# Second parts of weight pieces: by an accumulating transfer instead of a subtraction on VectorE

## The chip, the cores and the metric

The kernel runs on one core of one Trainium2 chip. The metric is the device time of one execution in microseconds (us), lower is better. Before the change the median of three runs is 1182.73 us (1181.46 to 1182.98).

## What is computed

A two-layer decoder trunk on 512 tokens of width 1024, all in float32. Cut to what matters:

```python
# layer 0
proj = x @ w_in                                  # q | k | v | g | a low-rank gate
o = gla_chunked(q, k, v, log_a)                  # 4 heads, gated linear attention
mix = (rms_norm(o) * norm_g * silu(g)) @ gla_w_o
# layer 1: 16 heads of 64, weights by stick-breaking
kv = h @ kv_w;  q = h @ sb_w_q
mix = stick_breaking_attention(q, k, v) @ sb_w_o
# both layers
h = layer_norm(ALPHA * h + mix)
h = layer_norm(ALPHA * h + relu(h @ w_up) ** 2 @ w_down)   # D_FF = 4096
```

## The kernel before

Matmuls run in a reduced-precision format (F32R), so each operand x is kept as two parts: a first part hi, which is x rounded to F32R, and a second part lo = x - hi. A product is then three matmuls: hi with hi, hi with lo, lo with hi (mm3, L91 to 95, and the loop at L306 in the multiplications described next). The work is cut into weight pieces of 128 partitions by 1024 columns, 512 KB. For each piece SyncE loads the raw weights (L64), ScalarE writes hi with a copy (L70), VectorE writes lo with a subtraction (L72). The tiles come from pools: three raw buffers, six hi and six lo. A piece can be made only when the matmuls of the piece six before it have read their buffers, so ScalarE's hi copy normally starts when TensorE lets a buffer go.

Three shapes of use follow. pieces_512 gives four pieces (two for half a weight), each two blocks of 128 rows by 512 columns; piece_128 gives one piece of eight blocks of 128 by 128. In the up half of the MLP (function up) TensorE goes through a piece once, 24 matmuls. In a row product (function rows, for values and gates) TensorE goes through all four pieces of a group once per block of tokens, four times, so the four are released together near the end of the group. The output products of the first mixer and of both MLPs (function seven) use seven products of sub-blocks instead of eight. Their weights are loaded ahead in eight B tiles (L266), which VectorE combines with each other in place (L335, L336, L346, L347). Six of the seven products take such tiles, two pieces each, of which the first two, split_b(2) and split_b(3) of L337 and L343, use tiles that are still plain weights. The other one, plain_b, loads its two pieces anew through raw. There are nine such multiplications, eight of them in the MLPs.

In the attention the heads go in eight pairs. GpSimd multiplies each of five weight tiles of a pair (w, L770) with the result of a scan on VectorE (r, L769), and copies keys across partitions (kh, L737). LayerNorm takes means and variances on VectorE, a power on GpSimd (rs, L185), the centring on VectorE (h, L189), and then TensorE transposes (L213) for the next product.

The code names no order between engines: a recording layer orders the instructions of each engine by its own estimate of when their inputs are ready, and inserts the waits. Each engine works its queue strictly in that order. GpSimd's queue also holds any DMA that it issues. In the lines below a name with a number, as in L72, is a line of the kernel before.

Of the kernel before, what the change touches and what calls it, by code (L numbers as in the profile page):

```python
# [8 lines left out]
F32 = mybir.dt.float32  # L9
F32R = mybir.dt.float32r  # L10
I32 = mybir.dt.int32
AF = mybir.ActivationFunctionType
ALU = mybir.AluOpType
# [21 lines left out]
def yoco_kernel(ctx: ExitStack, tc: tile.TileContext, x, gla_w_in, gla_w_a2, gla_b_a, gla_norm_g,  # L35
                gla_w_o, kv_w, sb_w_q, sb_w_o, mlp_w_up, mlp_w_down, ln_g, ln_b, out):
    nc = tc.nc
# [10 lines left out]
    def nm(s):  # L48
        uid[0] += 1
        return f"{s}{uid[0]}"  # L50

    def bank():
        return psp.tile([P, 512], F32, tag="b", name=nm("ps"))

    def row_tile():
        return big.tile([P, D], F32, tag="h", bufs=4, name=nm("h"))

    def unit(dtype):
        return big.tile([P, 4, 512], dtype, tag="T", bufs=8, name=nm("T"))


    def split_piece(src, a):
        raw = wts.tile([P, 1024], F32, tag="raw", bufs=3, name=nm("raw"))
        nc.sync.dma_start(out=raw.rearrange("p (a b) -> p a b", a=a), in_=src)  # L64
        return split_tile(raw, a)

    def split_tile(raw, a):
        v = lambda w: w.rearrange("p (a b) -> p a b", a=a)
        hi = wts.tile([P, 1024], F32R, tag="hi", bufs=6, name=nm("hi"))
        nc.scalar.activation(hi, raw, AF.Copy)  # L70
        lo = wts.tile([P, 1024], F32R, tag="lo", bufs=6, name=nm("lo"))
        nc.vector.tensor_tensor(lo, raw, hi.bitcast(F32), op=ALU.subtract)  # L72
        return v(hi), v(lo)

    def block(w, r0, c0):
# [21 lines left out]
    def put(hi, lo, ps, keep=lambda ins: ins):  # L97
        keep(nc.scalar.activation(hi, ps, AF.Copy))  # L98
        keep(nc.vector.tensor_tensor(lo, ps, hi.bitcast(F32), op=ALU.subtract))  # L99
# [154 lines left out]
    def seven(a1, a2, weights, pool, hs, fresh, norms=False, mid=None, narrow=False):  # L254
# [6 lines left out]
        a11, a21, a12, a22 = a1[:, :, lo_t], a1[:, :, hi_t], a2[:, :, lo_t], a2[:, :, hi_t]  # L261
        bs = []
# [9 lines left out]
        def split_a(a):  # L272
            u = unit(F32R)
            put(u[:, :, lo_t], u[:, :, hi_t], a)
            return lambda k, s: (u[:, k, 128 * s:128 * s + 128], u[:, k, 256 + 128 * s:384 + 128 * s])

        def split_b(i):
            got = []
            for h in range(2):
                hi, lo = split_tile(bs[h][i], 2)  # L280
                got += [(hi[:, 0, :], lo[:, 0, :]), (hi[:, 1, :], lo[:, 1, :])]
            return got

# [9 lines left out]
        ys, xs, zs = ([None, None] for _ in range(3))  # L293
# [28 lines left out]
        def product(*how, **more):  # L322
            for s in range(2):
                part(s, *how, **more)
# [9 lines left out]
        for b22, b12, b11, b21 in bs:  # L334
            tt(b22, b22, b12, op=ALU.subtract)  # L335
            tt(b12, b12, b11, op=ALU.subtract)  # L336
        product(split_a(a11), split_b(2), ys, True, False, 0, 0)  # L337
        if mid:
            mid()
            sums()  # L340
        q12 = split_a(a12)
        tt(a21, a11, a21, op=ALU.subtract)
        product(q12, split_b(3), xs, True, True, 0, 0, last=True)  # L343
        tt(a12, a12, s2, op=ALU.subtract)
        for b22, b12, b11, b21 in bs:
            tt(b11, b22, b11, op=ALU.add)  # L346
# [52 lines left out]
    xs, pss = [row_tile() for _ in range(NT)], [bank() for _ in range(NT)]  # L399
# [8 lines left out]
    for u in range(2):  # L408
        for t in range(NT):
            nc.sync.dma_start(out=xs[t][:, 512 * u:512 * u + 512],  # L410
                              in_=x2[128 * t:128 * t + 128, 512 * u:512 * u + 512])
# [3 lines left out]
            raw, hi, lo = (w[:, 512 * (t % 2):512 * (t % 2) + 512] for w in trio)  # L415
            k = 4 * u + t
# [185 lines left out]
    op = tc.tile_pool(name="gated", bufs=1, reuse_waits="tile")  # L602
# [120 lines left out]
    class Pair:  # L723
# [23 lines left out]
        def weights(self):  # L747

            self.ws = []
            for kind, segs in ((0, ((0, 3, 0),)), (1, ((0, 2, 0), (0, 0, 384))), (0, ((1, 3, 0),)),  # L750
                               (1, ((1, 2, 0), (1, 0, 384))), (2, ((0, 1, 0), (1, 1, 256)))):
                z = bank()
                for a, i, f in segs:
                    q = self.qs[:, a, P * i:P * i + P]
                    n = P * (i + 1)
                    for k, end in ((self.kh, False), (self.kl, True)):
                        nc.tensor.matmul(z[:, f:f + n], lhsT=q, rhs=k[:, a, 0:n], start=not end, stop=end)

                z4 = z.rearrange("p (b c) -> p b c", c=P)
                last = (z4[:, 3:4, :], z4[:, 2:4, :], z4[:, 1::2, :])[kind]  # L760
                nc.vector.tensor_tensor(last, last, low.unsqueeze(1).broadcast_to([P, last.shape[1], P]), op=ALU.add)  # L761
                r = sbp.tile([P, S + 1], F32, tag="r", bufs=3, name=nm("r"))
                w = chain()
                nc.gpsimd.memset(r[:, S:S + 1], 1.0)
                rb = r[:, 0:S]
                nc.scalar.activation(rb, z, AF.Sigmoid, scale=-1.0)
                nc.scalar.activation(w, z, AF.Sigmoid)
                down = rb[:, ::-1]
                nc.vector.tensor_tensor_scan(down, down, begins[kind][:, ::-1], 1.0, op0=ALU.mult, op1=ALU.max)  # L769
                nc.gpsimd.tensor_tensor(w, w, r[:, 1:S + 1], op=ALU.mult)  # L770
                self.ws.append((segs, w))
# [116 lines left out]
```

## Time and profile before

| | |
|---|---|
| median of 3 runs | 1182.73 us |
| the profiled execution's own time | 1182.95 us |
| its span, first to last instruction | 1181.0 us |
| TensorE busy | 1137.2 us (96%) |
| VectorE busy | 877.0 us (74%) |
| ScalarE busy | 546.5 us (46%) |
| GpSimd busy | 96.2 us (8%) |
| DMA engines' share by loads | 32.5% of 16 engines' span, 120.96 MB |

The profile is of one execution. PE is TensorE's matmuls, PEld its weight loads, DVE VectorE, ACT ScalarE, POOL GpSimd, SPq SyncE's queue, which issues the loads. A row of the groups names line, engine, operation, tiles (out<-in), shapes and count, then busy time in us and the mean in ns, then the engine's idle time just before, and what ended it. A row of the waits reads: who waited, for whom, us in total, times, longest. A row of the timeline starts with the start and the duration in us. A row of the DMA issues ends with the size and the median time from issue to landing.

### The profile page before, as it was taken

To read this page: it belongs to the slowest core of one execution; us is meant where nothing else is said; L and a number is where in the kernel's file an instruction comes from. 1 tells how busy PE (TensorE), PEld (TensorE's weight loads), DVE (VectorE), ACT (ScalarE), POOL (GpSimd) and SP (SyncE) were. 2 spreads that over 40 slices of the span, in tenths; PEclk is the share of its full clock that TensorE was granted. 3 is DMA by queue.
4 is the path that set the end of the run, shared out by engine and by line. 5 is a ranking of instruction groups with operands and counts; after the bars stand their busy time and mean duration, and the time that the engine had idled before them with its cause. 6 is when DMAs were issued, how large, how long until landed. Compare 5 with 4: busy or idle time off the path is not lost.

```text
span 1181.0 us, 14039 instructions
## 1 busy us (share of the span) xinstructions
PE 1137.2 (96%) x5401; PEld 934.0 (79%) x5401; DVE 877.0 (74%) x1053; ACT 546.5 (46%) x807; POOL 96.2 (8%) x159
## 2 busy tenths in 40 slices
PE   8999999799999999998799999999999999999986
PEld 7788887598888888886588877778988888888865
DVE  4577558985877857968953787786958768679697
ACT  4455435553433524534643667664544435345250
POOL 1011100000000000000010443431000000000001
PEclk9999998899999999998899999999999999999988
DMA  7441341272351450421243311111732614515101
GB/s 229 121 125 54 99 134 54 88 238 103 102 183 36 142 164 33 162 71 36 72 129 106 87 41 67 55 54 36 234 123 87 193 42 129 174 34 163 54 1 71
DMA packets 87846, 121.84 MB, mean 103 GB/s; under 512 B 11298, under 2 KB 37026, under 8 KB 87780
## 3 DMA queue, kind: packets, MB, share of 16 engines
q1 hardware_dynamic: 87780, 120.96, 32.5%
q8 instruction: 42, 0.69, 0.2%
q14 instruction: 24, 0.20, 0.1%
HBM read 118.85 MB, written 2.10 MB: 102 GB/s over the span
## 4 chain that ended last, share of the span: by engine, by line
PE 78%; DVE 15%; ACT 3%; issue 2%; POOL 1%; DMA 0%; SPq 0%; DVEq 0%; POOLq 0%; ACTq 0%
PE ps L306 26%; PE ps L93 16%; PE ps L94 16%; PE ps L95 16%; DVE r L769 4%; DVE lo L72 3%; ACT wt L784 1%; DVE T L99 1%; DVE h L168 1%; ACT hi L70 1%; DVE bst L176 1%; DVE ps L761 1%; DVE qs L744 1%; PE ps L213 1%; POOL rs L185 1%
## 5 line engine op out<-in xcount | busy, mean ns | idle before, releaser
L306 PE MATMUL ps<-hi,T 128*128 128x512 f32 (+1 forms) x1016 | 326.7, 399 | 16.4 <-ACT T L98 7.0
L93 PE MATMUL ps<-T,hi 128*128 128x512 f32 (+1 forms) x768 | 288.7, 376 | 0.0
L95 PE MATMUL ps<-T,lo 128*128 128x512 f32 (+1 forms) x768 | 285.5, 372 | 0.0
L94 PE MATMUL ps<-T,hi 128*128 128x512 f32 (+1 forms) x768 | 285.4, 372 | 0.0
L306 PEld LDWEIGHTS ps<-hi,T 128*128 128x128 f32 x1016 | 195.5, 194 | 64.6 <-ACT T L98 8.1
L72 DVE TENSOR_TENSOR lo<-raw,hi 128x1024 fp32r<-128x1024 f32 x134 | 163.0, 1225 | 111.3 <-ACT hi L70 107.6
L70 ACT ACTIVATE hi<-raw 128x1024 fp32r<-128x1024 f32 x134 | 142.6, 1065 | 191.7 <-PE ps L306 90.1
L306 PE MATMUL ps<-lo,T 128*128 128x512 f32 (+1 forms) x508 | 201.4, 396 | 0.0
L70 ACT ACTIVATE hi<-B 128x1024 fp32r<-128x1024 f32 x108 | 114.5, 1060 | 171.7 <-PE ps L94 99.4
L72 DVE TENSOR_TENSOR lo<-B,hi 128x1024 fp32r<-128x1024 f32 x108 | 131.1, 1222 | 64.1 <-ACT hi L70 63.5
L95 PEld LDWEIGHTS ps<-T,lo 128*128 128x128 f32 x768 | 144.7, 188 | 25.0
L93 PEld LDWEIGHTS ps<-T,hi 128*128 128x128 f32 x768 | 144.7, 188 | 24.6 <-issue 1.1
L94 PEld LDWEIGHTS ps<-T,hi 128*128 128x128 f32 x768 | 144.8, 189 | 23.5
L306 PEld LDWEIGHTS ps<-lo,T 128*128 128x128 f32 x508 | 98.4, 194 | 19.6
L93 PE MATMUL ps<-hi,T 128*128 128x512 f32 x256 | 103.1, 404 | 0.0
L95 PE MATMUL ps<-hi,T 128*128 128x512 f32 x256 | 100.8, 394 | 0.0
L94 PE MATMUL ps<-lo,T 128*128 128x512 f32 x256 | 100.8, 394 | 0.0
L168 DVE TENSOR_TENSOR h<-ps,h 128x512 f32<-128x512 f32 x109 | 74.6, 686 | 13.6 <-PE ps L306 9.5
L185 POOL TENSOR_TENSOR rs<-ve,mhalf 128x1 f32<-128x1 f32 x16 | 12.2, 760 | 814.2 <-DVE ve L183 814.2
L769 DVE TENSOR_TENSOR_SCAN r<-r,begin 128x512 f32<-128x512 f32 x40 | 66.2, 1663 | 0.2
L660 DVE TENSOR_TENSOR s<-ps,s 128x512 f32<-128x512 f32 x64 | 43.3, 688 | 19.4 <-ACT s L659 19.4
L770 POOL TENSOR_TENSOR w<-w,r 128x512 f32<-128x512 f32 x40 | 51.4, 1285 | 75.7 <-DVE r L769 60.5
(164 smaller groups left out, 1223.7 us busy)
## 6 DMA issues: line engine op xcount, KB each, us to landing
raw<-in_mlp_w_up_dram SPq DMA_DIRECT2D x64, 512.0 KB, 3.8
B<-in_mlp_w_down_dram SPq DMA_DIRECT2D x64, 512.0 KB, 4.0
raw<-in_gla_w_in_dram SPq DMA_DIRECT2D x20, 512.0 KB, 3.9
raw<-in_mlp_w_down_dram SPq DMA_DIRECT2D x16, 512.0 KB, 3.9
raw<-in_kv_w_dram SPq DMA_DIRECT2D x16, 512.0 KB, 3.9
B<-in_gla_w_o_dram SPq DMA_DIRECT2D x8, 512.0 KB, 7.2
raw<-in_sb_w_q_dram SPq DMA_DIRECT2D x8, 512.0 KB, 4.3
raw<-in_sb_w_o_dram SPq DMA_DIRECT2D x8, 512.0 KB, 3.5
```

What stands on the lines that cost most here:

```text
L70: nc.scalar.activation(hi, raw, AF.Copy)
L72: nc.vector.tensor_tensor(lo, raw, hi.bitcast(F32), op=ALU.subtract)
L93: nc.tensor.matmul(ps, lhsT=a[0], rhs=b[0], start=first, stop=False)
L94: nc.tensor.matmul(ps, lhsT=a[0], rhs=b[1], start=False, stop=False)
L95: nc.tensor.matmul(ps, lhsT=a[1], rhs=b[0], start=False, stop=last)
L99: keep(nc.vector.tensor_tensor(lo, ps, hi.bitcast(F32), op=ALU.subtract))
L168: nc.vector.tensor_tensor(h, ps, h, op=ALU.add)
L185: nc.gpsimd.tensor_tensor(rs, ve, mhalf[:, 0:1], op=ALU.pow)
L306: nc.tensor.matmul(banks[s][:, c], lhsT=a(k, s)[x], rhs=b[k][y][:, c], start=opens and (k, x, y) == (0, 0, 0), stop=closes and (k, x, y) = ...
L660: nc.vector.tensor_tensor(s2[:, f, :], pss[f], s2[:, f, :], op=ALU.mult)
L769: nc.vector.tensor_tensor_scan(down, down, begins[kind][:, ::-1], 1.0, op0=ALU.mult, op1=ALU.max)
L770: nc.gpsimd.tensor_tensor(w, w, r[:, 1:S + 1], op=ALU.mult)
```

## The change

Second parts of plain weights are no longer subtracted on VectorE. ScalarE writes a second copy of the raw weights, with the sign turned, into lo; since lo is an F32R tile, this is -hi. Then GpSimd issues a DMA that reads the same weights from memory again and adds them to lo in place, so that lo = weights - hi. This is done for all pieces through raw tiles (134) and for the two products of each of the nine multiplications whose B tiles are still plain (36 pieces). The other 72 B pieces, which VectorE has combined, keep the subtraction.

```diff
     def split_piece(src, a):
         raw = wts.tile([P, 1024], F32, tag="raw", bufs=3, name=nm("raw"))
         nc.sync.dma_start(out=raw.rearrange("p (a b) -> p a b", a=a), in_=src)
-        return split_tile(raw, a)
-
-    def split_tile(raw, a):
+        return split_tile(raw, a, src)
+
+    def split_tile(raw, a, src=None):
+
         v = lambda w: w.rearrange("p (a b) -> p a b", a=a)
         hi = wts.tile([P, 1024], F32R, tag="hi", bufs=6, name=nm("hi"))
         nc.scalar.activation(hi, raw, AF.Copy)
         lo = wts.tile([P, 1024], F32R, tag="lo", bufs=6, name=nm("lo"))
-        nc.vector.tensor_tensor(lo, raw, hi.bitcast(F32), op=ALU.subtract)
+        if src is not None:
+            nc.scalar.activation(lo, raw, AF.Copy, scale=-1.0)
+            nc.gpsimd.dma_start(out=v(lo), in_=src, accum_op=ALU.add)
+        else:
+            nc.vector.tensor_tensor(lo, raw, hi.bitcast(F32), op=ALU.subtract)
         return v(hi), v(lo)
...
-        def split_b(i):
+        def split_b(i, *block):
             got = []
             for h in range(2):
-                hi, lo = split_tile(bs[h][i], 2)
+                k, j = block or (0, 0)
+                hi, lo = split_tile(bs[h][i], 2, weights(k, h, j) if block else None)
                 got += [(hi[:, 0, :], lo[:, 0, :]), (hi[:, 1, :], lo[:, 1, :])]
             return got
...
-        product(split_a(a11), split_b(2), ys, True, False, 0, 0)
+        product(split_a(a11), split_b(2, 0, 0), ys, True, False, 0, 0)
...
-        product(q12, split_b(3), xs, True, True, 0, 0, last=True)
+        product(q12, split_b(3, 1, 0), xs, True, True, 0, 0, last=True)
```

The new instructions stand in the queues of ScalarE and GpSimd, and some old ones change places. First ScalarE's queue in the first MLP, at the end of a multiplication of seven products: the two pieces of plain_b (raw_2764, raw_2770), the last B pieces, and the first pieces of the next up group. Before:

```order
L70 ACTIVATE hi_2766<-raw_2764 128x1024
L70 ACTIVATE hi_2772<-raw_2770 128x1024
L98 ACTIVATE T_2802<-s_2287 128x4x256
L70 ACTIVATE hi_2805<-B_2578 128x1024
L70 ACTIVATE hi_2809<-B_2586 128x1024
L98 ACTIVATE T_2813<-s_2420 128x4x256
L70 ACTIVATE hi_2816<-B_2584 128x1024
L70 ACTIVATE hi_2820<-B_2592 128x1024
L70 ACTIVATE hi_2878<-raw_2876 128x1024
L70 ACTIVATE hi_2884<-raw_2882 128x1024
```

And now (the same raw tiles are numbered 2806, 2813 and 2920):

```order
L74 ACTIVATE lo_2810<-raw_2806 128x1024
L71 ACTIVATE hi_2808<-raw_2806 128x1024
L71 ACTIVATE hi_2815<-raw_2813 128x1024
L74 ACTIVATE lo_2817<-raw_2813 128x1024
L103 ACTIVATE T_2846<-s_2317 128x4x256
L71 ACTIVATE hi_2849<-B_2616 128x1024
L71 ACTIVATE hi_2853<-B_2624 128x1024
L103 ACTIVATE T_2857<-s_2454 128x4x256
L71 ACTIVATE hi_2860<-B_2622 128x1024
L71 ACTIVATE hi_2864<-B_2630 128x1024
L74 ACTIVATE lo_2924<-raw_2920 128x1024
L71 ACTIVATE hi_2922<-raw_2920 128x1024
```

A lo copy has come beside each hi copy of a raw piece; of two pieces that follow each other, the first has its lo copy ahead of its hi copy and the second behind it. The B pieces here are combined ones, and have none.

Next GpSimd's queue in the attention, from the fourth and fifth w of one head pair over the copies of keys (kh) to the first products of the next. Before:

```order
L770 TENSOR_TENSOR w_5019<-w_5019,r_5018 128x512
L764 MEMSET r_5200 128x1
L770 TENSOR_TENSOR w_5032<-w_5032,r_5031 128x512
L764 MEMSET r_5211 128x1
L737 COPY kh_5105<-kh_5105 64x512 x2
L770 TENSOR_TENSOR w_5188<-w_5188,r_5187 128x512
L764 MEMSET r_5224 128x1
L770 TENSOR_TENSOR w_5201<-w_5201,r_5200 128x512
L764 MEMSET r_5237 128x1
```

And now:

```order
L770 MEMSET r_5307 128x1
L75 DMA lo_5581<-in_sb_w_q_dram 128x8x128
L743 COPY kh_5200<-kh_5200 64x512
L75 DMA lo_5729<-in_kv_w_dram 128x8x128
L743 COPY kh_5200<-kh_5200 64x512
L776 TENSOR_TENSOR w_5284<-w_5284,r_5283 128x512
L770 MEMSET r_5320 128x1
L776 TENSOR_TENSOR w_5297<-w_5297,r_5296 128x512
L770 MEMSET r_5333 128x1
L75 DMA lo_5768<-in_sb_w_q_dram 128x8x128
L776 TENSOR_TENSOR w_5308<-w_5308,r_5307 128x512
```

Transfers stand between the two kh copies and ahead of the third w (in this pair, the first of its kind, also ahead of the kh copies; in the pairs behind it only at the other two places).

Last GpSimd's queue at the LayerNorm behind the first mixer, four token blocks, each with one power rs. Before:

```order
L185 TENSOR_TENSOR rs_1848<-ve_1846,mhalf 128x1
L185 TENSOR_TENSOR rs_1869<-ve_1867,mhalf 128x1
L185 TENSOR_TENSOR rs_1951<-ve_1949,mhalf 128x1
L185 TENSOR_TENSOR rs_2011<-ve_2009,mhalf 128x1
L185 TENSOR_TENSOR rs_4365<-ve_4363,mhalf 128x1
```

And now:

```order
L190 TENSOR_TENSOR rs_1874<-ve_1872,mhalf 128x1
L75 DMA lo_2073<-in_mlp_w_up_dram 128x2x512
L190 TENSOR_TENSOR rs_1895<-ve_1893,mhalf 128x1
L75 DMA lo_2080<-in_mlp_w_up_dram 128x2x512
L75 DMA lo_2087<-in_mlp_w_up_dram 128x2x512
L75 DMA lo_2094<-in_mlp_w_up_dram 128x2x512
L190 TENSOR_TENSOR rs_1977<-ve_1975,mhalf 128x1
L75 DMA lo_2330<-in_mlp_w_up_dram 128x2x512
L190 TENSOR_TENSOR rs_2037<-ve_2035,mhalf 128x1
```

The second to fourth rs now stand behind transfers, each of which waits for its own lo copy on ScalarE.

## The prediction

> **What bounds the kernel now.** I read the page's busy line first, then the waits of TensorE, then busy time by stretch.
>
> ```profile
> span 1181.0 us, 14039 instructions
> PE 1137.2 (96%) x5401; PEld 934.0 (79%) x5401; DVE 877.0 (74%) x1053; ACT 546.5 (46%) x807; POOL 96.2 (8%) x159
> PE ps L213 <- DVE h L189: 13.9, 6, 5.6
> PE ps L306 <- ACT T L98: 7.0, 3, 2.4
> PE ps L306 <- DVE T L99: 3.4, 3, 1.9
> PE ps L779 <- POOL w L770: 3.1, 5, 1.7
> 180.00:245.00 65.00, 55.07 (x251) 44.46 (x250) 60.06 (x81) 37.80 (x57) 2.87 (x4) 0.89 0.26 77
> 411.45:493.33 81.88, 81.88 (x361) 67.41 (x360) 61.73 (x64) 34.70 (x38) 0.00 (x0) 1.00 0.36 116
> 530.00:595.00 65.00, 53.37 (x224) 41.90 (x222) 59.40 (x79) 36.92 (x56) 3.31 (x7) 0.89 0.21 65
> 1120.00:1181.00 61.00, 46.57 (x196) 37.42 (x194) 52.04 (x78) 18.72 (x20) 3.66 (x4) 0.85 0.10 35
> ```
>
> TensorE is idle for only 43.8 of 1181.0 us, so nothing that speeds VectorE up can give more than that. The idle time sits where LayerNorm and the start of a product meet: 9.9 us in 180 to 245, 11.6 in 530 to 595, 14.4 in the last 61 (columns: length, then PE, PEld, DVE, ACT, POOL busy, clock, DMA share, GB/s). In the first two VectorE works 92% and 91% of the time, and the largest wait names it (L189, the centring). In one period of the MLP (411 to 493: one down product and two up groups) TensorE has no idle time, although VectorE has 20 us free. There a faster VectorE is worth nothing, and the change can only cost.
>
> **Part 1: the subtraction leaves VectorE.**
>
> ```profile
> L72 DVE TENSOR_TENSOR lo<-raw,hi 128x1024 fp32r<-128x1024 f32 x134 | 163.0, 1225 | 111.3 <-ACT hi L70 107.6
> L72 DVE TENSOR_TENSOR lo<-raw,hi 128x1024 fp32r<-128x1024 f32 x8 | 9.7, 1212 | 0.3 <-ACT hi L70 0.2
> L70 ACT ACTIVATE hi<-raw 128x1024 fp32r<-128x1024 f32 x134 | 142.6, 1065 | 191.7 <-PE ps L306 90.1
> ```
>
> The change touches all 134 pieces read through raw tiles and 36 of the 108 read through B tiles (two products of nine multiplications, two halves each): 170. VectorE loses 170 x 1.225 = 208 us. What counts is the two crowded stretches: 180 to 245 holds eight of the raw subtractions, 9.7 us (second row, of that stretch alone), against 4.9 us that VectorE now has free there; 530 to 595 holds about as many. The waits of TensorE for the centring, in these two stretches alone, are what it can give back:
>
> ```profile
> PE ps L213 <- DVE h L189: 6.0, 2, 4.9
> PE ps L213 <- DVE h L189: 6.9, 3, 5.6
> ```
>
> That is 12.9 us. I take two thirds of it, **-9 us**, between 0 (the centring also waits for GpSimd and for TensorE's own sums) and -13.
>
> **Part 2: a copy with the sign turned on ScalarE.** 170 x 1.06 us = 180 us, by the row of the hi copy, the same operation; ScalarE rises from 546 to 727 us. Over the whole it has room (37.8 of 65 us in the crowded stretch), but it works in order, and TensorE waits 7.0 us for its T copies at these places. Together with GpSimd's part (the rs powers of LayerNorm, L185, now stand behind a transfer's issue) I take **+2 us**, between 0 and 8.
>
> **Part 3: the transfer between the first part and the matmul.** Before, a second part is ready 2.3 us after the hi copy starts. Now a transfer of 512 KB stands there. The trace has none that accumulates, so it is bounded by its neighbours.
>
> ```profile
> raw<-in_mlp_w_up_dram SPq DMA_DIRECT2D x64, 512.0 KB, 3.8
> raw<-in_sb_w_q_dram SPq DMA_DIRECT2D x8, 512.0 KB, 4.3
> L64 SPq DMA_DIRECT2D raw<-in_kv_w_dram x16: 367/368/368, 509.3 to 675.4; - x16
> lnb<-in_ln_b_dram SPq DMA_DIRECT2D x4, 512.0 KB, 7.3
> ```
>
> The lower end is a plain load of the size, 3.8 us. In the MLP period 18 loads keep the DMA engines busy for 0.36 x 81.88 = 29.5 us, 1.64 us each. An accumulating transfer must also read what it adds to, so I price it as two loads, 3.3 us of the engines, between one and three. GpSimd must issue it: SyncE needs 0.37 us for a load, a whole load lands in 3.8, and between these I choose 1.5. So D, from the end of the ScalarE copy to the landing, is 3.8 + 1.6 + 1.5 = 7 us where the engines are free, between 3.8 and 12 (7.3, the slowest landing of this size, with two more reads and the issue). The Trainium skill ("Collectives: The Full Stack", section on the bandwidth ceiling and the fold count) says that a reducing transfer is slower because of its two source reads and not because of the add, and moves at half the rate of a copy. No run here shows it yet. By its half rate the 512 KB would take 3.3 us of the engines as well.
>
> Against D stands the lead: the time from when a buffer comes free (hi copy starts) to the first matmul that reads lo.
>
> ```profile
> 154.14 1.06 ACT L70 ACTIVATE hi<-raw 128x1024 fp32r<-128x1024 f32 x1 [0.73 <-PE ps L95]
> 161.47 0.39 PE L94 MATMUL ps<-lo,T 128*128 128x512 f32 x1
> 162.83 0.39 PE L94 MATMUL ps<-lo,T 128*128 128x512 f32 x1
> 609.00 1.06 ACT L70 ACTIVATE hi<-raw 128x1024 fp32r<-128x1024 f32 x1 [0.76 <-PE ps L95]
> 615.83 0.39 PE L94 MATMUL ps<-lo,T 128*128 128x512 f32 x1
> 617.19 0.39 PE L94 MATMUL ps<-lo,T 128*128 128x512 f32 x1
> 415.50 1.06 ACT L70 ACTIVATE hi<-raw 128x1024 fp32r<-128x1024 f32 x1 [3.02 <-PE ps L306]
> 425.38 0.39 PE L95 MATMUL ps<-T,lo 128*128 128x512 f32 x1
> 481.06 1.06 ACT L70 ACTIVATE hi<-raw 128x1024 fp32r<-128x1024 f32 x1 [0.23 <-PE ps L306]
> 494.69 0.39 PE L306 MATMUL ps<-lo,T 128*128 128x512 f32 x1
> ```
>
> Most pieces have 12 to 45 us and are safe. The tight ones are where a group of four follows another in six buffers. At the second value group of the attention, ScalarE now does lo, hi, hi, lo from 609.00, so the second lo ends at 613.24; with D = 7 it lands at 620.2 for a matmul that wanted it at 617.19: 3.1 us late. At the second gate group the same gives 154.14 + 4.24 + 7 = 165.4 against 162.83: 2.5 us. **+5.6 us** together, 0 with D = 4, 11.6 with D = 10.
>
> In the MLP the tightest is the first piece of the up group behind a down product: ready at 415.50 + 1.06 + D, wanted at 425.38, so it stalls from D = 8.8. Then come the two late plain pieces of a down product: the second is ready at 481.06 + 4.24 + D, wanted at 494.69, so it stalls from 9.4. These places are the ones where loads crowd:
>
> ```profile
> 399.00:434.00 35.00, 35.00 (x155) 28.60 (x154) 29.37 (x31) 15.41 (x15) 0.00 (x0) 1.00 0.58 186
> ```
>
> Loads take 0.58 x 35 = 20.3 us of the engines there, and the nine accumulating transfers that fall into the stretch add 9 x 3.3 = 30 us: 50 in 35. A backlog builds up, so for the first of them I take D = 10. That is 1.2 us at each of six up groups and 0.6 us at each of eight down products: **+12 us**, between 0 (D under 8.8) and 40 (D = 13). The up pieces behind them lead by 17 to 28 us and outlast the backlog.
>
> **Part 4: GpSimd's queue in the attention.** Per head pair two transfers, of 1024 rows of 512 B, stand between its products w and its kh copies.
>
> ```profile
> 717.69 1.09 POOL L770 TENSOR_TENSOR w<-w,r 128x512 f32<-128x512 f32 x1 [1.25 <-ACT w L767]
> 720.03 1.09 POOL L770 TENSOR_TENSOR w<-w,r 128x512 f32<-128x512 f32 x1 [1.09 <-DVE r L769]
> 722.37 1.09 POOL L770 TENSOR_TENSOR w<-w,r 128x512 f32<-128x512 f32 x1 [1.09 <-ACT hi L70]
> 724.71 1.90 POOL L770 TENSOR_TENSOR w<-w,r 128x512 f32<-128x512 f32 x1 [1.10 <-DVE r L769]
> ...
> 705.65 1.19 DVE L72 TENSOR_TENSOR lo<-raw,hi 128x1024 fp32r<-128x1024 f32 x1
> 705.90 1.90 POOL L770 TENSOR_TENSOR w<-w,r 128x512 f32<-128x512 f32 x1 [1.09 <-DVE r L769]
> 662.00:775.00 113.00, 111.52 (x608) 87.89 (x607) 90.88 (x103) 74.62 (x150) 47.42 (x69) 1.00 0.19 61
> ```
>
> One comes ahead of the third w. Idle time before the third, fourth and fifth is 1.25 + 1.09 + 1.10 = 3.4 us, so an issue of up to that length is made good before TensorE waits for the fifth. The other delays the second kh copy, which feeds only the third of the five scans. I take 2.5 us for an issue, and nothing on the path.
>
> **Sum.** The profiled execution took 1182.95 us, 1181.0 of span and 1.95 around it; the median of the three is 1182.73, so nothing is to be corrected. 1182.95 - 9 + 2 + 5.6 + 12 = 1193.6; I say **1193**. A measurement of this kernel tells about 0.2% from no change, 2.4 us.
>
> **Rivals.**
> *The transfers are quick* (D about 5, issue 1 us). Then the gate and value groups lose about 1.5 us, the MLP nothing, and VectorE's relief stays: 1182.95 - 9 + 2 + 1.5 = 1177, faster. For it speak the 3.8 us of a load and leads of 12 us and more at most pieces; against it, the DMA share of 0.58 where leads are short. Chance 0.26.
> *The DMA engines become the bound.* A period of 81.88 us has 29.5 us of loads and 14 accumulating transfers. At twice a load that is 29.5 + 46 = 75 us, which still fits; it stops fitting at 2.3 times. At 2.5 times it is 87 us, 5 us more in each of about seven periods, on top of the forecast 1230; at three times 98 us, 16.5 more, 1308. Chance 0.20.
> *GpSimd issues slowly.* The w at 705.90 took 1.90 us with VectorE's subtraction beside it, and the others 1.09: GpSimd's work can stretch by 1.7 beside VectorE, which is busy 90.88 of 113 us in the attention. If the issue of 1024 rows takes 8 us (twice the landing of a whole load), w falls 4.6 us behind in each of seven pairs, 32 us: 1225. The Trainium skill ("SBUF — State Buffer", section "SBUF: two separate sides") says that a transfer issued from GpSimd stands still while VectorE runs an operation in its two-port mode, since descriptors cannot be written, 620 ns becoming 3100; the trace agrees so far as w is slowed, and shows no transfer. Chance 0.15.
> *No effect by cancelling:* the edges of the forecast and of the first rival, below.
>
> **How the numbers follow.** Forecast 0.39 (own range 1183 to 1206), quick 0.26, DMA-bound 0.20, slow issue 0.15. Faster by over 0.2% is the quick rival with its upper edge taken off and a little of the forecast: 0.27. Within 0.2% (1180.4 to 1185.1): 0.12, from these edges. The rest is slower, 0.61. The range leaves out the part of the quick rival under 1174 and the DMA-bound one from about 2.8 times on: 1174 to 1260.
>
> **What would show it.** Right: the waits of TensorE in 180 to 245 and 530 to 595 for L189 shrink; new waits of TensorE for lo, named with the accumulating transfer, appear at the second gate and value groups and behind the down products, 1 to 3 us each; D reads about 7 us in the DMA issues and 10 in the MLP. Wrong: D under 6 and no TensorE wait for lo (quick), DMA share over 0.9 through the MLP (engines), or w waiting behind transfers in GpSimd's queue, with TensorE waiting for w (issue).

## The result, and the profile after

The median went from 1182.85 us (four runs) to **1214.84 us** (1213.11 to 1216.71), a ratio of 1.0274 with a 95% interval of 1.0256 to 1.0291: 32 us slower, where 10 were forecast. The page of the changed kernel: span, busy times, GpSimd's DMA queue (q0), and issues with the median time to landing.

```profile
span 1212.6 us, 14495 instructions
PE 1148.4 (95%) x5401; PEld 938.0 (77%) x5401; DVE 680.2 (56%) x883; ACT 699.9 (58%) x977; POOL 309.4 (26%) x329
q0 software_dynamic: 64672, 89.14, 44.1%
raw<-in_mlp_w_up_dram SPq DMA_DIRECT2D x64, 512.0 KB, 9.0
lo<-in_mlp_w_up_dram POOLq DMA_DIRECT2D x64, 512.0 KB, 9.9
lo<-in_mlp_w_down_dram POOLq DMA_DIRECT2D x48, 512.0 KB, 8.8
lo<-in_gla_w_in_dram POOLq DMA_DIRECT2D x20, 512.0 KB, 9.2
```

VectorE lost 197 us (208 forecast) and ScalarE gained 153 (180 forecast). A transfer lands 9 to 10 us after its issue in the three groups shown (6.0 to 10.0 in the four smaller ones). The raw load of an up piece, which took 3.8 us, now takes 9.0 beside the transfers. The waits of TensorE:

```profile
PE ps L218 <- DVE h L194: 9.9, 4, 4.2
PE ps L312 <- ACT T L103: 9.8, 5, 2.4
PE ps L99 <- DMA lo<-in_gla_w_in_dram: 9.4, 4, 4.5
PE ps L100 <- DMA lo<-in_mlp_w_up_dram: 6.9, 5, 3.2
PE ps L99 <- DMA lo<-in_kv_w_dram: 5.1, 3, 2.4
PE ps L312 <- DVE T L104: 4.5, 3, 1.9
...
PE ps L312 <- DMA lo<-in_mlp_w_down_dram: 2.2, 5, 0.7
```

Lines have moved by five or six here (L218 was L213, L312 was L306). The wait for the centring fell from 13.9 to 9.9, the waits for T grew from 7.0 and 3.4 to 9.8 and 4.5, and the waits for lo are new, 23.6 us in all. The waits for w (3.1 us before) are gone.

TensorE runs 5401 matmuls in each of these kernels. The end of the k-th, less its end in the kernel before, tells where time goes (k counts from 0). The table is worked out from the traces; e1, e2, e4 and e7 are experiments below.

```
   k  place                        before us  after    e1    e2    e4    e7
 120  start                             31.5   -1.0   0.1  -1.5  -1.1  -0.8
 360  second value group done           86.7    7.0   0.1  -1.5  -1.1  -0.8
 720  in the gates                     152.3    6.8   0.2  -1.8  -1.1  -1.0
 840  end of the gates                 177.3   13.3   0.2  -1.8  -1.1  -1.0
1320  first LayerNorm done             277.9   14.2  -4.1  -1.7   0.9  -0.3
2400  first MLP                        523.4   17.6  -3.6  -1.2   3.9   1.5
2640  second LayerNorm done            592.3   19.8  -3.0   0.4   4.7   3.3
2880  values of the attention done     646.6   27.0  -3.8  -0.4   4.7   3.8
3840  attention done                   830.6   23.7  -8.0  -4.6   3.1   0.6
3960  first up group of second MLP     846.0   27.6  -9.1  -5.7   3.1   5.9
5400  last matmul                     1173.7   31.5  -9.4  -4.8   3.9   9.8
```

So the changed kernel loses 8 us in the start's second value group, 6.5 in the second gate group, 7.2 in the value groups of the attention, 3.9 at the first up group of the second MLP, and 3.4 and 3.9 in the rest of the two MLPs. It loses 0.9 and 2.2 around the two LayerNorms behind the mixer and the first MLP, and wins 3.3 in the attention.

Waits for lo are only part of these losses. The timeline of TensorE at the second gate group (start, duration; in brackets the idle time before):

```profile
167.56 0.39 PE L99 MATMUL ps<-lo,T 128*128 128x512 f32 x1
...
168.01 0.39 PE L98 MATMUL ps<-hi,T 128*128 128x512 f32 x1
170.78 0.51 PE L99 MATMUL ps<-lo,T 128*128 128x512 f32 x1 [2.38 <-DMA lo<-in_gla_w_in_dram]
...
171.94 0.63 PE L99 MATMUL ps<-lo,T 128*128 128x512 f32 x1
...
174.41 0.77 PE L99 MATMUL ps<-lo,T 128*128 128x512 f32 x1 [0.98 <-DMA lo<-in_gla_w_in_dram]
```

Three stretches of the same trace follow, behind the wait, after it, and behind a wait of 3.23 us at the first up group of the second MLP. The columns are those of the prediction: length, PE, PEld, DVE, ACT and POOL busy, granted clock, DMA share, GB/s. (The DMA share counts each packet whole in the stretch where it starts, so that of a short stretch can exceed 1.)

```profile
171.00:178.00 7.00, 6.02 (x17) 4.32 (x17) 0.38 (x1) 0.83 (x2) 0.00 (x0) 0.51 1.12 220
178.00:185.00 7.00, 7.00 (x34) 5.81 (x33) 1.38 (x4) 1.92 (x4) 0.00 (x0) 1.00 0.11 16
869.30:876.00 6.70, 6.69 (x56) 6.70 (x57) 0.00 (x0) 1.02 (x2) 0.00 (x0) 1.00 1.10 273
```

TensorE waits 2.38 and 0.98 us, 3.4 together, but the group ends 6.5 us later. From 171 to 178 the same matmul takes 0.63 us where it took 0.39, and the granted clock is 0.51: behind the wait TensorE runs some 7 us at half the clock. Over the whole span TensorE's busy time rose from 1137.2 to 1148.4 us with the same matmuls, and its idle time from 43.8 to 64.2. The 31.6 us of the spans are 20.4 of standing still and 11.2 of more busy time. That is matmuls at half the clock and, in part, lost overlap: matmuls of 0.39 us start 0.23 us apart, and the first one behind a wait overlaps none. The Trainium skill ("TensorE: Matmul & The Clock Gate", section "Why this matters for your kernels") warns of idle gaps over about 3 us between bursts; here a gap of 2.4 us was enough at one place, and at 869 us a gap of 3.23 us left the clock at 1.00.

### The profile page after: what moved, and what is told of

Its sections match the earlier page's. It is cut to its first block, busy times and chain, and to the rows that moved or that the text cites. A ratio compares the mean times of both kernels' runs of the same rounds, so it can differ in the third digit from the quotient of the medians.

```text
span 1212.6 us, 14495 instructions
## 1 busy us (share of the span) xinstructions
PE 1148.4 (95%) x5401; PEld 938.0 (77%) x5401; DVE 680.2 (56%) x883; ACT 699.9 (58%) x977; POOL 309.4 (26%) x329
## 3 DMA queue, kind: packets, MB, share of 16 engines
q1 hardware_dynamic: 87780, 120.96, 32.3%
## 4 chain that ended last, share of the span: by engine, by line
PE 74%; DMA 11%; issue 7%; DVE 3%; ACT 3%; POOL 1%; SPq 0%; POOLq 0%; DVEq 0%; ACTq 0%
PE ps L98 17%; PE ps L99 17%; PE ps L100 17%; PE ps L312 17%; DMA lo<-in_mlp_w_down_dram 4%; DMA lo<-in_mlp_w_up_dram 3%; PE ps L763 2%; PE ps L799 2%; DMA lo<-in_kv_w_dram 2%; DMA lo<-in_gla_w_in_dram 1%; PE ps L785 1%; ACT hi L71 1%; DMA raw<-in_sb_w_q_dram 1%; ACT lo L74 1%; POOL lo L75 1%
## 5 line engine op out<-in xcount | busy, mean ns | idle before, releaser
L312 PE MATMUL ps<-hi,T 128*128 128x512 f32 (+1 forms) x1016 | 328.2, 400 | 19.3 <-ACT T L103 9.8
L312 PEld LDWEIGHTS ps<-hi,T 128*128 128x128 f32 x1016 | 196.1, 194 | 68.9 <-ACT T L103 11.7
L312 PE MATMUL ps<-lo,T 128*128 128x512 f32 (+1 forms) x508 | 202.4, 398 | 2.3 <-DMA lo<-in_mlp_w_down_dram 2.2
L71 ACT ACTIVATE hi<-raw 128x1024 fp32r<-128x1024 f32 x134 | 138.3, 1053 | 102.9 <-DMA raw<-in_mlp_w_up_dram 43.0
L74 ACT ACTIVATE lo<-raw 128x1024 fp32r<-128x1024 f32 x134 | 141.2, 1054 | 73.7 <-PE ps L312 63.0
L75 POOL DMA_DIRECT2D lo<-in_mlp_w_up_dram x64 | 76.7, 1199 | 249.4 <-ACT lo L74 232.1
L75 POOL DMA_DIRECT2D lo<-in_mlp_w_down_dram x48 | 58.3, 1215 | 277.9 <-PE ps L312 160.1
L77 DVE TENSOR_TENSOR lo<-B,hi 128x1024 fp32r<-128x1024 f32 x72 | 88.0, 1222 | 53.5 <-ACT hi L71 53.5
L312 PEld LDWEIGHTS ps<-lo,T 128*128 128x128 f32 x508 | 98.7, 194 | 24.6 <-ACT hi L71 3.6
L99 PE MATMUL ps<-lo,T 128*128 128x512 f32 x256 | 103.4, 404 | 14.5 <-DMA lo<-in_gla_w_in_dram 9.4
L98 PE MATMUL ps<-hi,T 128*128 128x512 f32 x256 | 104.7, 410 | 0.0
L100 PE MATMUL ps<-hi,T 128*128 128x512 f32 x256 | 102.5, 400 | 0.0
L352 DVE TENSOR_TENSOR B<-B,B 128x1024 f32<-128x1024 f32 x18 | 22.0, 1223 | 89.3 <-ACT lo L74 89.3
L99 PEld LDWEIGHTS ps<-lo,T 128*128 128x128 f32 x256 | 49.6, 194 | 27.8 <-issue 6.7
```

The lines of the kernel that those rows point to most:

```text
L74: nc.scalar.activation(lo, raw, AF.Copy, scale=-1.0)
L75: nc.gpsimd.dma_start(out=v(lo), in_=src, accum_op=ALU.add)
L98: nc.tensor.matmul(ps, lhsT=a[0], rhs=b[0], start=first, stop=False)
L99: nc.tensor.matmul(ps, lhsT=a[0], rhs=b[1], start=False, stop=False)
L100: nc.tensor.matmul(ps, lhsT=a[1], rhs=b[0], start=False, stop=last)
L312: nc.tensor.matmul(banks[s][:, c], lhsT=a(k, s)[x], rhs=b[k][y][:, c], start=opens and (k, x, y) == (0, 0, 0), stop=closes and (k, x, y) = ...
```

## The experiments

Theory A: transfers that land late, where a group of four wants them at once, stop TensorE and then its clock, and VectorE's relief is worth next to nothing. Theory B, the rival of the first four runs: the relief is worth the forecast 9 us, and the transfers cost about 41. Theory C, the rival later: the transfers cost through contention, by slowing the raw loads and filling GpSimd's queue, wherever lo is read. Each ratio is to runs of the kernel before that were taken beside the experiment: their median is 1183.46 us for e1 to e4, 1183.65 for e5 to e8 and 1183.03 for e9 to e11.

**e1_no_lo.** No second parts for plain pieces at all.

```diff
+        if src is not None:
+            return v(hi), v(hi)
```

> Leaves out the second parts of the 170 plain pieces altogether (TensorE reads the first part twice): no copy on ScalarE, no transfer, no subtraction on VectorE, the same matmuls. Theory A (the 32 us come from landings that are late for TensorE, and from the half clock that follows such a stall; freeing VectorE is worth almost nothing, since the idle time at LayerNorm is a chain of short steps): 1178 to 1183 us. Theory B (freeing VectorE is worth the 9 us that were forecast, and the transfers cost 41): 1170 to 1175 us.

Measured 1171.21 us, a ratio of 0.9894 (0.9865 to 0.9923). The relief exists, 12 us by the medians and 9.4 by the spans (the runs lie between 1167.3 and 1174.3, and the trace is of one at 1173.3): theory A falls on this point, and B's 1170 to 1175 holds. The waits of TensorE in it:

```profile
PE ps L219 <- DVE h L195: 9.8, 4, 4.2
PE ps L313 <- ACT T L104: 7.3, 3, 2.6
...
PE ps L313 <- DVE T L105: 2.7, 4, 1.2
```

The wait for the centring falls by 4.1 us and no further, since it has GpSimd's rs and VectorE's own chain left in it. The wait for w in the attention (3.1 us before) is gone. The table shows 4.3 us won around the first LayerNorm, nothing around the second, and 4.2 in the attention.

**e2_copy_only.** ScalarE makes the second copy, nothing is added to it.

```diff
             nc.scalar.activation(lo, raw, AF.Copy, scale=-1.0)
-            nc.gpsimd.dma_start(out=v(lo), in_=src, accum_op=ALU.add)
```

> Keeps ScalarE's second copy and leaves out the accumulating transfer, so that lo is the negative of the first part. Theory A: 1179 to 1185 us, no wait of TensorE for a transfer, no half clock beyond what it was before. Theory B: 1172 to 1178. If ScalarE's copies carry the cost: 1190 or more.

Measured 1177.85 us, 0.9952 (0.9937 to 0.9967). That is again in B's range (1172 to 1178). Half of the relief goes back to ScalarE's copies, and TensorE's waits name them:

```profile
PE ps L311 <- ACT T L102: 9.8, 5, 2.4
PE ps L311 <- DVE T L103: 4.9, 3, 1.9
```

The wait for the centring is as in e1 (9.8), and the waits for T have grown from 7.3 and 2.7 to 9.8 and 4.9: 4.7 us, against 4.6 between the spans of e1 and e2. The copies stand ahead of the T copies in ScalarE's queue. The transfers then cost 1214.84 - 1177.85 = 37 us.

**e3_plain_transfer.** The transfer overwrites lo instead of adding to it.

```diff
-            nc.gpsimd.dma_start(out=v(lo), in_=src, accum_op=ALU.add)
+            nc.gpsimd.dma_start(out=v(lo), in_=src)
```

> The same transfers from GpSimd, at the same places, but plain (lo is overwritten with the weights): same issue on GpSimd, same waits, one read instead of two. If the engines' time of the accumulation makes the landings late: landings at 6 to 7 us and 1190 to 1202 us. If it is the issue and the way through GpSimd: landings at 8 us or more and 1208 to 1215 us.

Measured 1189.72 us, 1.0054 (1.0035 to 1.0072). A plain transfer in the same place costs 12 us over e2, the accumulation another 25. The time lies just under the range for a cost by the engines' time (1190 to 1202), and the range for the issue and the way through GpSimd (1208 to 1215) falls. Its queue and landing on the page:

```profile
q0 software_dynamic: 64672, 89.14, 29.8%
lo<-in_mlp_w_up_dram POOLq DMA_DIRECT2D x64, 512.0 KB, 6.6
lo<-in_mlp_w_down_dram POOLq DMA_DIRECT2D x48, 512.0 KB, 4.1
lo<-in_gla_w_in_dram POOLq DMA_DIRECT2D x20, 512.0 KB, 5.7
```

Per transfer that is 0.298 x 1190.1 / 170 = 2.09 us of the engines, against 0.441 x 1212.6 / 170 = 3.15 with accumulation. In these groups landing takes 4 to 7 us against 9 to 10. The cost is not proportional: TensorE waits for lo four times over 1 us in this trace and eight times in that of the changed kernel.

**e4_groups_subtract.** The groups of four (values, gates, the attention's output product, the first up group of each MLP; 36 pieces) go back to the subtraction.

```diff
-    def pieces_512(w, r0, nkt, c0):
+    def pieces_512(w, r0, nkt, c0, add=False):
...
-            hi, lo = split_piece(block(w, r0 + 256 * kp, c0), 2)
+            hi, lo = split_piece(block(w, r0 + 256 * kp, c0), 2, add)
...
-            pcs = pieces_512(mlp_w_up[l], 0, 8, 512 * g)
+            pcs = pieces_512(mlp_w_up[l], 0, 8, 512 * g, g > 0)
```

> Subtraction on VectorE for the pieces that are used in groups of four (values, gates, output of the attention, and the first up group of each MLP), transfers for all others. Theory A: the stalls at the start (8 us by first uses), the gates (5), the values (7) and the first up group of the second MLP (3) go with their half clock, the MLP's 7 stay: 1186 to 1193 us. If the cost is the DMA engines' load as a whole: over 1200.

Measured 1187.87 us, 1.0039 (1.0025 to 1.0053): 27 of the 32 us sit in 36 of the 170 pieces, as theory A expected (1186 to 1193). In the table the steps at 360, 840, 2880 and 3960 are gone, and 3.0 us in the first MLP and 0.8 in the second stay.

**e5_nobody_waits.** All copies and transfers, but TensorE reads hi in place of lo.

```diff
-        return v(hi), v(lo)
+        return v(hi), v(hi if src is not None else lo)
```

> Left out of the computation: the matmuls read hi in place of lo for the 170 plain pieces, so the second parts of these weights do not enter the products. ScalarE's second copies and all 170 accumulating transfers are still made, but TensorE waits for none of them. The kernel with the copies alone took 1177.85 us, the changed one 1214.84: the transfers cost 37 us. Theory A (the landing comes late and TensorE waits for lo, with the lower clock behind each wait): all of the 37 us go, 1178 us (1175 to 1182), and TensorE's idle time is that of the kernel with the copies alone, about 40 us. Theory C (contention: the raw loads land in 9.0 us where they took 3.8, GpSimd's queue holds rs and w up, whoever waits for lo): 1190 us or more, with TensorE waiting for hi or for raw loads in the place of lo.

Measured 1225.26 us, 1.0351 (1.0335 to 1.0367): slower than the changed kernel. The number lies in theory C's range (1190 or more) and outside A's (1175 to 1182). But C's sign, TensorE waiting for hi or raw loads, does not show: TensorE waits for results of ScalarE and VectorE, and ScalarE waits for the landings. First ScalarE's waits, then its timeline where keys and queries of the attention begin, then TensorE's waits:

```profile
ACT lo L74 <- DMA raw<-in_mlp_w_up_dram: 60.2, 23, 11.1
ACT lo L74 <- DMA lo<-in_mlp_w_up_dram: 47.3, 15, 4.3
```

```profile
677.51 1.06 ACT L74 ACTIVATE lo<-raw 128x1024 fp32r<-128x1024 f32 x1 [10.83 <-DMA raw<-in_sb_w_q_dram]
678.59 0.59 ACT L749 ACTIVATE qs<-ps 64x512 fp32r<-64x512 f32 x1
```

```profile
PE ps L312 <- ACT T L103: 17.9, 5, 6.7
...
PE ps L763 <- DVE qs L750: 6.2, 1, 6.2
```

A lo that nobody reads depends on no matmul, so its copy moves up in ScalarE's queue. There it stands until the raw tile, or the transfer into the same buffer six pieces earlier, has landed, and qs and T stand behind it. The run doesn't tell A from C, since it changed the order as well as the wait. It shows that the same landings do as much harm on ScalarE's queue as on TensorE's.

**e6_attention_only.** Transfers for keys and queries alone.

```diff
-    def piece_128(w, c0):
+    def piece_128(w, c0, add=False):
...
-            ps = cols(h2T, piece_128(kv_w, P * self.p))
+            ps = cols(h2T, piece_128(kv_w, P * self.p, True))
...
-            ps = cols(h2T, piece_128(sb_w_q[0], P * self.p), mid)
+            ps = cols(h2T, piece_128(sb_w_q[0], P * self.p, True), mid)
```

> The transfers are kept for the 16 pieces of keys and queries in the attention alone, the other 154 go back to VectorE's subtraction. By the k-th matmul of each trace, the changed kernel gains 3.3 us between the start of the attention's pairs and the last block of tokens of it (it lies 27.0 us behind the kernel before at matmul 2880 and 23.7 at 3840), and the kernel without second parts 4.2 there. If this gain is the attention's own: 1180 us (1178 to 1182), a ratio of 0.997. If it came from buffers and loads that earlier delays had let run ahead: 1183 us or more, no change.

Measured 1180.76 us, 0.9977 (0.9967 to 0.9987): as expected, and faster than both kernels. By the k-th matmul the trace loses 1.9 us at the first pieces (2880 to 3000) and wins 2.8 behind them.

**e7_lo_last.** In the three groups at 360, 840 and 2880 of the table, three blocks of tokens go through all of hi before the first matmul with lo. The number of matmuls, copies, transfers and loads is that of the changed kernel.

```diff
+    def ahead(sp, pcs):
+        pss = [bank() for _ in range(3)]
+        for t, ps in enumerate(pss):
+            for k in K8:
+                a = sp.k(k, 128 * t, 128)
+                nc.tensor.matmul(ps, lhsT=a[0], rhs=pcs[k][0], start=k == 0, stop=False)
+                nc.tensor.matmul(ps, lhsT=a[1], rhs=pcs[k][0], start=False, stop=False)
+        return pss
...
-    def rows(sp, t, pcs, ks):
+    def rows(sp, t, pcs, ks, pss=()):

+        if t < len(pss):
+            for k in K8:
+                a = sp.k(k, 128 * t, 128)
+                nc.tensor.matmul(pss[t], lhsT=a[0], rhs=pcs[k][1], start=False, stop=k == 7)
+            return pss[t]
         ps = bank()
```

> The changed kernel, with the matmuls put in another order in three groups of four (the second value group of the start, the second gate group, the second value group of the attention): the first three blocks of tokens go through all eight blocks of hi (48 matmuls) before the first matmul that reads lo, so that lo has some 10 us more to land; transfers, copies and loads stay as they are. The trace of the changed kernel falls behind by 8, 6.5 and 7 us at these three places. Theory A (late landing): about 20 of the 32 us go, less about 1 at each end: 1196 us (1193 to 1200). Theory C (contention for engines and queues): the order of the matmuls changes nothing of it, 1210 us or more.

Measured 1193.5 us, 1.0073 (1.0056 to 1.0090): 21 us of the 32 go with nothing but an order of matmuls. Theory A holds and C falls for these groups. What e7 does not tell is why the pieces are late: the loads and transfers beside each other can be the reason. Of the waits for lo of values and gates one of 1.1 us is left, at the first value group of the attention, and the up pieces remain:

```profile
PE ps L218 <- DVE h L194: 9.9, 4, 4.2
...
PE ps L100 <- DMA lo<-in_mlp_w_up_dram: 5.2, 3, 3.8
```

**e8_before_lo_last.** The same edit in the kernel before.

> The control of the one above: the same order of the matmuls in the kernel before, with VectorE's subtraction. There TensorE waits for lo nowhere in these groups, so both theories expect no change, 1183 us (1181 to 1186). If it gains as much as the changed kernel gains by it, the gain is the order's own and says nothing of the transfers.

Measured 1183.15 us, 0.9992 (0.9983 to 1.0001). The order by itself is worth nothing; what e7 won, it won from the transfers.

**e9_pairs_2_to_7.** The attention's transfers without those of the first two pairs.

```diff
-            ps = cols(h2T, piece_128(kv_w, P * self.p, True))
+            ps = cols(h2T, piece_128(kv_w, P * self.p, self.p > 1))
...
-            ps = cols(h2T, piece_128(sb_w_q[0], P * self.p, True), mid)
+            ps = cols(h2T, piece_128(sb_w_q[0], P * self.p, self.p > 1), mid)
```

> As the kernel with transfers in the attention alone (1180.76 us), but the keys and queries of the first two pairs are subtracted on VectorE as well; 12 transfers are left. By the k-th matmul that kernel loses 1.9 us between matmul 2880 and 3000, where these first pieces are made, and wins 2.8 behind it. If the loss is the first pieces' own: 1179 us (1177 to 1181), 0.996. If the gain needs every pair, or the loss comes from the order of the start: 1181 us or more.

Measured 1179.9 us, 0.9976 (0.9965 to 0.9988). In the trace the loss of 1.9 us at the first pieces is gone and the gain of 2.8 stays. The medians of e6 and e9 differ by less than their intervals, so that the first pieces cost something is told by the trace alone. Together with e6 it is the fastest version here that leaves nothing out, 0.24% below the kernel before.

**e10_gpsimd_subtracts.** As e9, with six subtractions around the first LayerNorm on GpSimd.

```diff
-            nc.vector.tensor_tensor(lo, raw, hi.bitcast(F32), op=ALU.subtract)
+            (eng or nc.vector).tensor_tensor(lo, raw, hi.bitcast(F32), op=ALU.subtract)
...
-                hi, lo = split_tile(bs[h][i], 2, None)
+                hi, lo = split_tile(bs[h][i], 2, None, nc.gpsimd if fresh and norms and block else None)
...
-                hi, lo = split_piece(weights(k, h, j), 2)
+                hi, lo = split_piece(weights(k, h, j), 2, False, nc.gpsimd if fresh and norms else None)
```

> As the kernel with 12 transfers, and the six plain pieces of the first mixer's output product get their subtraction on GpSimd in place of VectorE, with neither a second copy on ScalarE nor a transfer. The kernel without second parts won 4.1 us between matmul 840 and 1080, where the first LayerNorm lies, the one with ScalarE's copies nothing there. If the crowd of VectorE's work is what counts there: 2 to 4 us below its sister, 1176 us. If a subtraction of 128x1024 on GpSimd (two to four times the 1.09 us of its 128x512 product) holds up rs of LayerNorm in GpSimd's queue or comes too late for the product: no gain or a loss of 1 to 5 us, 1180 to 1184 us.

Measured 1184.46 us, 1.0012 (1.0003 to 1.0021): 4.6 us more than e9 and just past the loss that the expectation allowed (1180 to 1184). By the k-th matmul it falls 5.7 us behind between 840 and 1080, around the first LayerNorm, where e9 loses nothing. GpSimd's group of the whole run, VectorE's timeline, and its group from 178 to 250 us:

```profile
L77 POOL TENSOR_TENSOR lo<-B,hi 128x1024 fp32r<-128x1024 f32 x4 | 10.4, 2631 | 29.0 <-ACT hi L71 15.3 <-PE ps L99 13.7
```

```profile
202.29 2.70 DVE L104 TENSOR_TENSOR T<-T,T 128x1024 fp32r<-128x1024 f32 x1
...
206.11 2.24 DVE L104 TENSOR_TENSOR T<-T,T 128x1024 fp32r<-128x1024 f32 x1
```

```profile
L353 DVE TENSOR_TENSOR B<-B,B 128x1024 f32<-128x1024 f32 x2 | 4.5, 2308 | 3.9 <-POOL lo L77 3.9
```

And VectorE's T subtractions of that stretch in e9:

```profile
L104 DVE TENSOR_TENSOR T<-T,T 128x1024 fp32r<-128x1024 f32 x6 | 7.2, 1219 | 0.0
```

GpSimd takes 2.6 us for a subtraction that VectorE does in 1.2, and VectorE pays twice. It waits 3.9 us until GpSimd is done with the B tiles that it combines in place. And of its six T subtractions the four that run alone take 1.22 us, while the two that meet GpSimd's (two subtractions from 201.50 to 207.26 us) take 2.70 and 2.24: each ends some 1.1 us behind one of GpSimd's. TensorE's wait for the centring there is 8.6 us, against 6.0 in e9. The work that was taken from VectorE came back as lateness and slower work on VectorE.

**e11_lo_last_up.** As e7, and the first up group of each MLP too.

```diff
+                if g == 0 and c0 == 0:
+                    for k in range(8):
+                        for f in range(4):
+                            nc.tensor.matmul(pss[f][:, :256], lhsT=pcs[k][1][:, 128 * f:128 * f + 128],
+                                             rhs=hT.k(k, 0, 256)[0], start=False, stop=k == 7)
```

> The changed kernel with the matmuls in three groups of four in the other order (1193.5 us), and now the first up group of each MLP as well: for the first half of the tokens all 64 matmuls with hi come ahead of the 32 that read lo. In its trace TensorE waits 4.4 us for lo at the first up group of the second MLP and 0.8 at that of the first. Theory A (late landing, lower clock behind it): 5 to 8 us less, 1187 us (1185 to 1190), with no wait for lo of an up group over 1 us. Theory C: no change, 1193.

Measured 1190.01 us, 1.0062 (1.0045 to 1.0078): 3.5 us less, where 5 to 8 were expected, and one wait for lo stays. (The 0.8 us that the expectation puts at the first MLP stand, in e7's trace, at a later up group of the second, at 1025.9 us.) The wait of TensorE, and the issue in GpSimd's timeline that it waits for:

```profile
PE ps L687 <- DMA lo<-in_mlp_w_up_dram: 2.7, 1, 2.7
```

```profile
841.75 1.19 POOL L75 DMA_DIRECT2D lo<-in_mlp_w_up_dram  x1 [5.12 <-ACT lo L74]
```

The last transfer of this group is issued late. GpSimd waits 5.12 us for ScalarE's second copy, and this order of the matmuls does not bring that copy forward.

## Why the prediction was wrong in size

The direction, the kind of places and the price of one transfer held. The step that failed is Part 3: when, and at which places, a late second part stops TensorE. The transfers were to cost 17.6 us (5.6 at two groups, 12 in the MLPs) and cost 37 (e2 against the changed kernel). By place the trace gives other numbers for every term.

**The relief, -9 for the LayerNorms: failed, and its size met by luck.** It was read as two thirds of the wait for the centring. That wait fell by 4.0 us, in every kernel without these subtractions (9.8 to 9.9 left). The 9.4 us of e1's trace are 4.1 of this wait, 3.1 of the waits for w in the attention, which Part 1 had left out, 0.4 of the waits for T, and 1.8 of TensorE's busy time (1137.2 to 1135.4 us). In the changed kernel nothing of it is left at the LayerNorms: they cost 0.9 and 2.2 us more than before.

**ScalarE's copies, +2: too small.** e2 against e1 prices them at 6.6 us by the medians and 4.6 by the spans. The step that TensorE already waits for T at these places was the right one to follow; the bound of 8 held.

**The transfer's price: held. D, 7 us where the engines are free: right there, but not where it was used.** 3.15 us of the engines per transfer stand against the 3.3 of the forecast, and the issue took 1.20 us against 1.5. A load takes 1.66 (0.325 x 1181.0 us for 120.96 MB). The Trainium skill's half rate ("Collectives: The Full Stack", the section on the bandwidth ceiling) agrees with 3.15 against 1.66; against the 2.09 of a plain transfer in the same place (e3) it is 1.5 times, so like for like this case shows less than the half rate says. The quickest transfers have a D of 6 us. But the engines are not free where groups meet. The buffers that release a transfer release raw loads too. The issues of the second gate group, of which the second lands for the matmul at 174.41, and the copies that they follow:

```profile
160.68 1.07 ACT L74 ACTIVATE lo<-raw 128x1024 fp32r<-128x1024 f32 x1 [0.50 <-PE ps L99]
...
163.55 1.04 ACT L74 ACTIVATE lo<-raw 128x1024 fp32r<-128x1024 f32 x1
```

```profile
162.04 1.22 POOL L75 DMA_DIRECT2D lo<-in_gla_w_in_dram  x1 [10.94 <-PE ps L99]
164.89 1.20 POOL L75 DMA_DIRECT2D lo<-in_gla_w_in_dram  x1 [1.63 <-PE ps L99]
```

From the end of the copy to the matmul, D is 170.78 - 161.75 = 9.0 and 174.41 - 164.59 = 9.8 us. The prediction's own line for D = 10 says 11.6 us for the second gate and value groups, and they lost 13.7 by the table. TensorE stood still for 8.4 of these; the other 5.3 went by in slower and less overlapped matmuls, which the prediction's line does not have.

**Most pieces "have 12 to 45 us and are safe": failed for one group.** The start's second value group had no row in the prediction. It lost 8 us, the largest single loss. In the trace of before, its fourth piece leads by 9.2 us only:

```profile
33.91 1.06 ACT L70 ACTIVATE hi<-raw 128x1024 fp32r<-128x1024 f32 x1 [1.55 <-DMA raw<-in_gla_w_in_dram]
...
43.06 0.39 PE L94 MATMUL ps<-lo,T 128*128 128x512 f32 x1
```

The page of the stretch from 36 to 52 us of the changed kernel shows why the transfers take long there: the DMA engines are busy throughout, in all 40 slices.

```profile
DMA  9999999999999999999999999999999999999999
```

The loads take long too. The raw load of that piece landed 8.5 us after its issue, where before it took 4.9. ScalarE waits for it, makes three T copies between hi and lo, and only then can the transfer start, which takes 8.4 us:

```profile
36.62 1.06 ACT L71 ACTIVATE hi<-raw 128x1024 fp32r<-128x1024 f32 x1 [3.05 <-DMA raw<-in_gla_w_in_dram]
...
39.02 1.07 ACT L74 ACTIVATE lo<-raw 128x1024 fp32r<-128x1024 f32 x1
```

So what makes lo late here is in part the contention that theory C names; how the 8 us divide is not measured. The first up group of the second MLP, 3.9 us, was missed as well: its second copies come late out of ScalarE's queue, between the copies of the LayerNorm (e11), and the two transfers that TensorE waits for have a D of 9 and 10 us.

**The MLPs, +12 by a backlog: half right.** First up groups apart, they lost 3.4 and 3.9, 7.3 together. D is about 10 there, as taken, but the waits are smaller and fewer: 2.4 us at three up groups for the forecast 7.2 at six, and 2.2 at five down products for 4.8 at eight. Busy time by stretch, of a run of up groups, of a period of the MLP and of the attention (columns as above):

```profile
262.00:345.00 83.00, 83.00 (x433) 71.48 (x431) 47.91 (x53) 48.26 (x58) 14.33 (x12) 1.00 0.92 231
427.00:510.00 83.00, 82.58 (x363) 67.61 (x362) 46.07 (x50) 47.62 (x52) 16.71 (x14) 1.00 0.85 203
...
680.00:795.00 115.00, 115.00 (x626) 92.34 (x628) 76.76 (x96) 94.37 (x172) 72.12 (x89) 1.00 0.77 139
```

In the period the DMA engines are busy 85% of the time, and TensorE still works 82.58 of 83 us; over the up groups they are busy 92%, and TensorE works throughout. There is a price, but no bound.

**GpSimd's queue in the attention, 0: held.** TensorE has no idle time from 680 to 795. Its waits for w (3.1 us before) are gone, and the trace wins 3.3 us. That is VectorE's relief, which Part 1 had left out there: e1 and e2 win 4.2 us without any transfer, e6 and e9 2.8 with transfers there alone.

**The clock: not in the sum at all.** A third of the loss, 11.2 of 31.6 us, is added busy time: matmuls at the lower clock behind the waits, and lost overlap. No run changed the clock alone, so how the 11.2 divide is open; the granted clock of 0.51 behind the wait, the matmuls' durations, and e7, where the busy time goes with the waits, speak for the clock. The page of e7:

```profile
span 1190.8 us, 14494 instructions
PE 1141.3 (96%) x5401; PEld 935.3 (79%) x5401; DVE 679.7 (57%) x883; ACT 699.8 (59%) x977; POOL 309.0 (26%) x329
```

The three groups held 13.7 us of waits for lo (6.0, 3.4 and 4.3). Without them the span is 21.8 us shorter, 14.7 of idle time and 7.1 of TensorE's busy time.

**The rivals.** The engines as the bound: no, though the share comes near; it is 0.83 to 0.92 through the MLPs, where the sign was over 0.9, and TensorE is not held up by it. A slow issue on GpSimd: no, 1.2 us, and 1.56 for 1024 rows, beside a VectorE busy 67% of the attention. Quick transfers: e3 shows what that would have been, and even there the time is 6 us above the kernel before.

**Two readings of the prediction that do not come out.** By its own line D = 13 costs the MLPs 54 us, not 40 (six times 4.2 and eight times 3.6). And the 1.25 us in its sum of idle time stand ahead of the second w; ahead of the third to fifth there are 3.3 us. Neither is in the forecast sum.

## What to carry to other kernels

Price a transfer that replaces an engine's instruction by its landing among the loads that the same event releases, and compare it with the lead of every group, the first one included. Expect TensorE to lose more to a wait than the wait itself: here 20.4 us of added idle time came with 11.2 us of added busy time, 1.5 times on the whole, and from 0.9 to 1.9 times at the four largest places, since the clock fell behind some waits and not behind others. Where a late operand can't be made earlier, the matmuls that don't need it can be put ahead of it, at no cost (e7, e8).

## What the runs showed of the hardware

- A 512 KB transfer from GpSimd's queue takes 2.09 us of the 16 engines plain and 3.15 us accumulating (a load from SyncE's queue 1.66), landing in 4 to 7 and 6 to 10 us by the groups' medians; its issue takes 1.20 us, or 1.55 with 1024 rows.
- Behind a wait of TensorE of 2.4 us the granted clock was 0.51 for 7 us, and matmuls took 0.63 us instead of 0.39. Behind a wait of 3.23 us, in the same trace, it stayed at 1.00.
- GpSimd's 128x1024 subtraction takes 2.6 us, and VectorE's two-operand work that meets it takes 2.24 and 2.70 us instead of 1.22. The Trainium skill ("SBUF — State Buffer", section "SBUF: two separate sides") says that the two engines share a pair of ports that one instruction holds alone, while the other waits; this run agrees, since VectorE's stretched work ends some 1.1 us behind GpSimd's (e10).
